# Slots found per 128 with the one-hot matrix as the stationary side, and x stored to DRAM once, tile by tile

## The chip, the cores and the metric

One core of a Trainium2 chip runs the whole program. The metric is the device time of one execution in microseconds (us). The kernel before takes 1715.98 us, the median of three runs (1715.34 to 1718.17).

## The reference

Two transformer layers run one after the other on 512 tokens of width 1024, in fp32. The change touches only the end of the second layer, a mixture of 32 experts in 4 groups of 8. Each token goes to one group and to two experts of it:

```python
def hier_moe(h, w_rg, b_rg, w_re, b_re, w_g, w_u, w_d):
    g_logits = hf @ w_rg + b_rg
    _, g_sel = lax.top_k(g_logits, 1)
    ...
    top_val, top_idx = lax.top_k(e_logits_sel, EXPERT_TOPK)     # 2 of the group's 8
    e_weight = softmax(top_val) * g_weight
    gates = sum(one_hot(e_idx, 32) * e_weight)                  # [tokens, 32]
    ...
        hid = silu(hf @ w_g[e]) * (hf @ w_u[e]) * gates[:, e]   # [tokens, 256] for each expert e
        out = out + hid @ w_d[e]
```

The layer's result is x + hier_moe(rmsnorm(x)).

## The kernel before, in words

Everything ahead of the experts (mixers, feed-forward part, the projection `out_proj(w_o2)`) leaves x, 512 tokens of 1024 fp32 numbers, in SBUF as four tiles of 128 tokens (index t). `out_proj` works in two column halves c = 0 and 1. DVE adds each tile's result to x and DVE or ACT squares it (`xsq`, `xss`) for the norm. After a half, `logits(c)` (L1379) transposes x on TensorE, ACT copies the result out of PSUM (`xT`), and TensorE multiplies it with the router's weights (`psB`). At its end two DMAs of POOL's queue (L1394 and L1395) send the half, 1 MB each: one to `x3d`, a copy of x in DRAM that the experts' tokens are fetched from, and one to `out`, which the experts' results are added to later.

Then the pools of the projection are closed, `x` among them, and the room is given to expert weights and to the pool `fn3`, in which the router works. `norm_r` (L658) begins the router with `nv<-xss` on DVE and makes 1/rms (`rsy`); the router turns logits into two experts for each token and a place for each of its two choices (`dest`, L1510). 32 experts have 64 places each, 2048 places in all, worked on in 16 passes q of 128 places (two experts). Of every token the table `tab` (L1528, six columns per token and choice) holds token number, weight and 1/(2 rms). `ogd` (L1552) is a small table for a branch of overfull experts that is not taken here.

`experts` (L1554) then has these parts:

- `slots(c)` (L1578) finds for 256 places which token lies there. For every t DVE compares a row 0..255 (`io`) with `dest`, first for the one choice (`oa`, L215) and then for both (`oh`, L210): 0/1 matrices of 128 tokens by 256 places. TensorE multiplies `tab` (stationary, six columns) by them, ACT copies the 6x256 result (`s6`, printed as `s`), TensorE turns it into two 128x6 pieces, and DVE writes token number `si`, weight `wt` and scale `rs`.
- `gather(q)` (L1566): POOL's indirect DMA fetches 128 rows of `x3d` into `xg`. Two such buffers are cleared once ahead of it (L1562).
- `turn(q)`: eight transposes of `xg` on TensorE (`pslin`, L242), which DVE spreads into `XT` (L207).
- `up(q)` (L1608): 32 matmuls `psA<-gu,XT`; ACT and DVE then make the hidden values `th`.
- `down(q)` (L1619): two transposes of `th` (`pspr<-cc,th`), ACT copies them (`hT`), 16 matmuls `psB<-dn,hT`, copies `y`, and POOL's indirect DMA adds `y` to `out` (L1632).

The engines run their instructions in the order in which the code issues them. Ahead of the loop stand slots(0), gather(0), gather(1), slots(1), turn(0), gather(2). A round q of the loop (L1641) is up(q), turn(q+1), gather(q+3), down(q-1), and in every second round slots(q/2 + 2) at its end.

Expert weights come over SP's queue in one fixed order: `gu` (1 MB each, four to a pass, 18 buffers, L1415) and `dn` (512 KB each, four to a pass, 6 buffers, L1420). A transfer into a used buffer waits on SP until the matmuls of its old content are done, dn number n for the down of number n-6, and whatever stands behind it on SP waits too.

Of the kernel before, what the change touches and what calls it, by code (L numbers as in the profile page):

```python
# [21 lines left out]
NT = 4  # L22
# [48 lines left out]
def constants():  # L71
    p = np.arange(128)
    t, q = p[:, None], p[None, :]
    same = (t // 64) == (q // 64)
    c = {"ident": np.eye(128), "t128": t <= q}
    t64, q64 = t % 64, np.arange(64)[None, :]
    c1 = {"tri": same & (t <= q), "gc": np.concatenate([t % 64 < q % 64, t % 64 <= q % 64], axis=1)}
    for l, n in SOLVE:
        b = 2 ** (l - 1)
        near = t64 // (b << n) == q64 // (b << n)  # L80
        c1["lv%d" % l] = near & ((t64 // b < q64 // b) if l == 1 else (t64 // b > q64 // b))
    c1["blk"] = same
    c1["id64"] = (t % 64) == np.arange(64)[None, :]
    c1["hsel"] = (t // 64) == np.arange(2)[None, :]
    tt = 128 * (3 - np.arange(4))[None, :, None] + p[:, None, None]
    c5 = {}
    c5["cm"] = ((tt - 16 * np.arange(31)[None, None, :] - 31) >= 0).reshape(128, 124)
    c2 = {}
    for l in range(7):
        n = 2 ** l  # L90
        c2["sl%d" % n] = (t // (2 * n) == q // (2 * n)) & (t % (2 * n) < n) & (q % (2 * n) >= n)
    c4 = {"up": np.where(q > t, -BIG, 0.0)}
    c3 = {"io": np.broadcast_to(np.arange(256)[None, :], (128, 256)), 
          "tok": t + 128 * np.arange(4)[None, :] + 1,
          "ts128": t < q, "ps64": np.broadcast_to(64.0 * (16 * (np.arange(32) // 16) + 2 * (np.arange(32) % 8) + np.arange(32) // 8 % 2)[None, :], (128, 32)),
          "rv": np.broadcast_to(8.0 - np.arange(8)[None, :], (128, 8))}
    out = {}
    for name, d in (("cc", c), ("cc1", c1), ("cc2", c2), ("cc3", c3), ("cc4", c4), ("cc5", c5)):
        at, parts = 0, []
        for k, v in d.items():  # L100
            v = np.asarray(v, np.float32)
            CCOL[k] = (name, at, v.shape[1])
            at += v.shape[1]
            parts.append(v)
        out[name] = np.concatenate(parts, axis=1)
    dist = 511 - np.arange(1024)
    bk = t5_thresholds()[np.clip(dist, 0, 511)]
    oh = np.zeros((33, 1024), np.float32)
    ok = (dist >= 0)
    oh[bk[ok], np.nonzero(ok)[0]] = -1.0  # L110
    oh[32, ~ok] = BIG
    sel = np.zeros((8, 4, 128), np.float32)
    for i in range(4):
        sel[2 * i, i, :64] = 1
        sel[2 * i + 1, i, 64:] = 1
    out["onehot"] = oh
    out["sel8"] = sel.reshape(8, 512)
    return out
# [70 lines left out]
class Kern:  # L189
# [1171 lines left out]
    def moe(self):  # L1361
        nc, tc, I = self.nc, self.tc, self.I
        with ExitStack() as s3:
# [5 lines left out]
            with tc.tile_pool(name="x3p", bufs=1) as xp:  # L1369
# [3 lines left out]
                nc.gpsimd.dma_start(bb, I["b_rt"].to_broadcast([128, 36]))  # L1373
                self.tt(wr, wr, self.pc("n2", 0, 8)[:, :, None].to_broadcast([128, 8, 36]))
                x3 = self.x
                ov = self.out.rearrange("(t p) d -> p t d", p=128)
                Lg = xp.tile([128, NT, 36], F32, name="Lg")

                def logits(c):  # L1379
                    psr = self.pt("B")  # L1380
                    for t in range(NT):
                        ps = self.pt("A")
                        for k in range(4):
                            self.tr(ps[:, k * 128:(k + 1) * 128], x3[:, t, (4 * c + k) * 128:(4 * c + k + 1) * 128])
                        xT = xp.tile([128, 4, 128], F32, name="xT", tag="xT", bufs=2)
                        self.copy("a", xT, ps.rearrange("p (k t) -> p k t", k=4))
                        for k in range(4):
                            self.mm(psr[:, t * 36:(t + 1) * 36], xT[:, k, :], wr[:, 4 * c + k, :], k == 0, k == 3)
# [2 lines left out]
                        self.copy("v", Lg, p3)  # L1391
                    else:
                        self.tt(Lg, p3, Lg, ALU.add)
                    for d in (self.x3d.rearrange("(t p) d -> p t d", p=128), ov):  # L1394
                        nc.gpsimd.dma_start(d[:, :, c * 512:(c + 1) * 512], x3[:, :, c * 512:(c + 1) * 512])  # L1395

                ss = self.out_proj(I["w_o2"], self.oT, xp, after=logits)
                self.dump("x3", x3)
                self.expert_load(2)
                self.rstack.close()  # L1400
                self.mw.append(L("mw2", side="right"))
# [151 lines left out]

    def experts(self, me):  # L1554
        nc = self.nc
        si = me.tile([128, 16], I32, name="si")
        wt = me.tile([128, 16], F32, name="wt")
        rs = me.tile([128, 16], F32, name="rs")
        TH, XT = {}, {}
        xg = [me.tile([128, D], F32, name="xg%d" % j) for j in range(2)]  # L1560
        for x in xg:
# [13 lines left out]
                        self.tr(ps[:, k * 128:(k + 1) * 128], xg[q % 2][:, (4 * c + k) * 128:(4 * c + k + 1) * 128])  # L1575
                    self.spread(XT[q], ps, c)

        def slots(c):  # L1578
            if c > 7:
                return  # L1580
            dc = me.tile([128, 2, NT], F32, name="dc", tag="dc", bufs=2)
            self.ts(dc, self.dest, -256.0 * c, None, op0=ALU.add)
            oh = [[None] * NT, [None] * NT]
            for t in range(NT):
                a = me.tile([128, 256], F32R, name="oa", tag="oa", bufs=2)
                self.ts(a, self.cc("io"), dc[:, 0, t:t + 1], None, op0=ALU.is_equal)
                o = me.tile([128, 256], F32R, name="oh", tag="oh", bufs=4)
                self.stt(o, self.cc("io"), dc[:, 1, t:t + 1], a.bitcast(F32), ALU.is_equal, ALU.add)
                oh[0][t], oh[1][t] = a, o
            ps = self.pt()  # L1590
            for k in range(2):
                for t in range(NT):
                    self.mm(ps[0:6, 0:256], self.tab[:, k, t, :], oh[k][t], k == 0 and t == 0, k == 1 and t == NT - 1)
            s6 = me.tile([6, 256], F32, name="s6", tag="s6", bufs=1)
            self.copy("a", s6, ps[0:6, 0:256])
            ps = self.pt()
            for q in range(2):
                self.tr(ps[:, q * 6:q * 6 + 6], s6[:, q * 128:(q + 1) * 128])
            qs = slice(2 * c, 2 * c + 2)
            st = me.tile([128, 2, 6], F32, name="st", tag="st", bufs=2)  # L1600
            self.copy("v", st, ps[:, 0:12].rearrange("p (q f) -> p q f", q=2))
            self.tt(rs[:, qs], st[:, :, 3], st[:, :, 4], ALU.add)
            self.tt(wt[:, qs], st[:, :, 1], st[:, :, 2], ALU.add)
            e = me.tile([128, 2], F32, name="e2", tag="e2", bufs=2)
            self.ts(e, st[:, :, 0], 0.0, 1.0e5, ALU.is_equal, ALU.mult)
            self.stt(si[:, qs], st[:, :, 0], -1.0, e, ALU.add, ALU.add)

        def up(q):  # L1608
            ps = self.pt("A")
# [22 lines left out]
            nc.gpsimd.indirect_dma_start(out=self.out, out_offset=bass.IndirectOffsetOnAxis(ap=si[:, q:q + 1], axis=0),  # L1632
                                         in_=y, in_offset=None, bounds_check=T - 1, oob_is_err=False, compute_op=ALU.add)

        slots(0)
        gather(0)
        gather(1)
        slots(1)
        turn(0)
        gather(2)  # L1640
        for q in range(16):  # L1641
            up(q)
            self.expert_load(3, 4 * q + 4, 4 * q - 4)
            turn(q + 1)
            gather(q + 3)
            if q:
                down(q - 1)
                self.expert_load(3, 4 * q + 4, 4 * q)
            if q % 2 == 0:
                slots(q // 2 + 2)  # L1650
        down(15)

    def spread(self, dst, ps, c):
# [55 lines left out]
```

## Time and profile before

| | us |
|---|---|
| median of three runs | 1715.98 |
| the profiled execution | 1718.04 |
| its span in the trace | 1716.3 |
| expert stage: first matmul of up(0) to end of the last weight transfer | 1465.75 to 1689.31 |
| TensorE busy | 1575.3 (92% of the span) |
| DVE busy | 938.0 (55%) |
| all DMA engines, mean over the span | 136 GB/s |

Times inside the execution are us from the span's start. PE is TensorE, SP the engine that issues weight transfers. The queue q1 carries the transfers that SP issues, q0 those of POOL. Names such as `oa`, `th` or `gu` are the program's tiles, and `r` is any of the router's small tiles; `L238` and the like are often lines of a helper (matmul, transpose, copy), so that a tile's name tells more than its line.

### The profile page before, as it was taken

Reading aid. Unit: us, or ns where it says so; the run is one execution under the profiler, and the core shown is the slowest. Engines: PE = TensorE matmul, PEld = TensorE weight load, DVE = VectorE, ACT = ScalarE, POOL = GpSimd, SP = SyncE. Lnnn points to the kernel's source line nnn. Section 1 sums busy time; section 2 is a strip of 40 time slices with the busy share of each in tenths; the row PEclk is TensorE's granted clock in tenths of the full one; section 3 lists DMA queues with packets and bytes.
Section 4 is the critical chain, followed back from the end, with each engine's and each line's share of the span. In section 5 each row is a group of like instructions: output and inputs, shape, how many; then the busy total and the mean of one; then the engine's idle time right before and its main releaser. Section 6 shows DMA issues by size and latency. Waiting matters only on the chain. (4 is left out here: it accounts for less than half of the span.)

```text
span 1716.3 us, 25176 instructions
## 1 busy us (share of the span) xinstructions
PE 1575.3 (92%) x9529; PEld 1108.7 (65%) x9529; DVE 938.0 (55%) x2227; ACT 558.4 (33%) x1130; POOL 297.5 (17%) x237
## 2 busy tenths in 40 slices
PE   6999999998899999999999999689888995999986
PEld 4678687868666678888888887467665473333321
DVE  4666766136587443877777234498487625323210
ACT  3432322334344333444444232334333431111100
POOL 3520101523111143000000000132032032212111
PEclk7899999999799999999999999799999997999998
DMA  5110111632221342222223333522212276799996
GB/s 185 58 60 15 52 60 48 212 102 68 83 74 53 104 158 88 92 93 97 94 93 94 96 92 94 149 72 94 68 38 69 111 266 264 275 366 367 409 401 215
DMA packets 88326, 233.06 MB, mean 136 GB/s; under 512 B 12131, under 2 KB 16707, under 8 KB 79756
## 3 DMA queue, kind: packets, MB, share of 16 engines
q1 hardware_dynamic: 78464, 206.70, 34.6%
q0 software_dynamic: 5856, 12.83, 2.8%
q10 hardware_dynamic: 3884, 11.91, 2.0%
q8 instruction: 76, 1.25, 0.3%
q14 instruction: 46, 0.38, 0.1%
HBM read 216.90 MB, written 22.09 MB: 139 GB/s over the span
## 5 line engine op out<-in xcount | busy, mean ns | idle before, releaser
L207 POOL TENSOR_TENSOR lo<-raw,hi 128x512 fp32r<-128x512 f32 (+1 forms) x152 | 199.3, 1314 | 994.7 <-ACT hi L219 891.5
L219 ACT ACTIVATE hi<-raw 128x512 fp32r<-128x512 f32 (+1 forms) x314 | 197.5, 631 | 432.7 <-PE pslin L238 193.1
L238 PE MATMUL pslin<-hhi,hi 128*128 128x512 f32 x696 | 281.9, 405 | 3.4 <-ACT hi L219 3.4
L238 PE MATMUL pslin<-hhi,lo 128*128 128x512 f32 x696 | 281.6, 405 | 1.5 <-POOL lo L207 1.5
L238 PE MATMUL pslin<-hlo,hi 128*128 128x512 f32 x696 | 282.4, 406 | 0.0
L207 DVE TENSOR_TENSOR lo<-raw,hi 128x512 fp32r<-128x512 f32 x162 | 111.3, 687 | 116.1 <-ACT hi L219 115.6
L238 PEld LDWEIGHTS pslin<-hhi,lo 128*128 128x128 f32 x696 | 132.7, 191 | 36.9 <-issue 3.7
L238 PEld LDWEIGHTS pslin<-hhi,hi 128*128 128x128 f32 x696 | 132.9, 191 | 35.7 <-ACT hi L219 4.3
L238 PEld LDWEIGHTS pslin<-hlo,hi 128*128 128x128 f32 x696 | 132.7, 191 | 32.5 <-issue 3.1
L238 PE MATMUL psA<-gu,XT 128*64 128x512 f32 x512 | 127.0, 604 | 12.7 <-DMA gu<-in_egu_dram 12.0
L238 PEld LDWEIGHTS psA<-gu,XT 128*64 128x64 f32 x512 | 37.9, 138 | 88.4 <-issue 63.1
L238 PE MATMUL psB<-dn,hT 128*64 128x512 f32 x256 | 72.4, 602 | 5.9 <-ACT hT L201 3.8
L210 DVE SCALAR_TENSOR_TENSOR u<-lr,pcol,u 128x511 f32<-128x511 f32 x88 | 65.9, 749 | 8.2 <-ACT u L219 6.6
L207 DVE TENSOR_TENSOR lr<-pslin,Rb 128x512 f32<-128x512 f32 x54 | 37.3, 690 | 51.3 <-PE pslin L238 44.0
L238 PE MATMUL pslin<-lo,hhi 128*128 128x512 f32 (+1 forms) x144 | 54.8, 381 | 2.9 <-DVE lo L207 2.8
L238 PE MATMUL pspr<-hi,hhi 128*128 128x512 f32 (+1 forms) x144 | 54.7, 382 | 1.7 <-ACT hq L219 1.7
L238 PE MATMUL pslin<-hi,hhi 128*128 128x512 f32 (+1 forms) x144 | 55.6, 387 | 0.0
L210 DVE SCALAR_TENSOR_TENSOR th<-th,psA 128x256 f32<-128x256 f32 x16 | 6.7, 418 | 88.5 <-ACT th L219 88.5
L238 PE MATMUL pspr<-lo,hhi 128*128 128x512 f32 (+1 forms) x144 | 54.3, 377 | 0.0
L238 PE MATMUL pspr<-hi,hlo 128*128 128x512 f32 (+1 forms) x144 | 54.2, 376 | 0.0
L238 PE MATMUL pslin<-hi,hlo 128*128 128x512 f32 (+1 forms) x144 | 53.9, 375 | 0.0
L219 ACT ACTIVATE th<-psA,rs 128x256 f32<-128x256 f32 x16 | 7.6, 474 | 136.6 <-PE psA L238 136.6
(652 smaller groups left out, 3046.6 us busy)
## 6 DMA issues: line engine op xcount, KB each, us to landing
gu<-in_egu_dram SPq DMA_DIRECT2D x64, 1024.0 KB, 16.1
dn<-in_ed_dram SPq DMA_DIRECT2D x64, 512.0 KB, 9.5
raw<-in_w_up_dram SPq DMA_DIRECT2D x88, 256.0 KB, 2.6
raw<-in_w_dn_dram SPq DMA_DIRECT2D x44, 256.0 KB, 2.6
raw<-in_w_g_dram SPq DMA_DIRECT2D x32, 256.0 KB, 2.6
raw<-in_w_o_dram SPq DMA_DIRECT2D x32, 256.0 KB, 2.7
raw<-in_w_a_dram SPq DMA_DIRECT2D x32, 256.0 KB, 2.6
raw<-in_w_rw_dram SPq DMA_DIRECT2D x28, 256.0 KB, 2.6
```

The source lines that it names most:

```text
L207: return (eng or self.nc.vector).tensor_tensor(out, a, b, op=op)
L210: return self.nc.vector.scalar_tensor_tensor(out, a, s, b, op0=op0, op1=op1)
L219: return self.nc.scalar.activation(out, in_, f, **k)
L238: return self.nc.tensor.matmul(out, lhsT=lhsT, rhs=rhs, start=start, stop=stop)
```

## The change

The x stores become eight ACT DMAs of one 128x512 tile each, issued inside `logits` ahead of that tile's transposes, and they go to `x3d` alone. `out` is filled once after `out_proj` by a DMA of POOL's queue from `x3d` (DRAM to DRAM, 2 MB). `slots(q)` now works for one pass of 128 places: the one-hot matrix (128x128) is the stationary side and `tab`'s six columns are the moving side, so that the result has places on the partitions and DVE reads it from PSUM with no copy and no transposes. The tiles of `slots` (`dc`, `oa`, `oh`, `e2`, `st`, `si`, `wt`, `rs`) move from the pool `me`, which is opened at the experts' start, to the pool `mh`, which is older and lies on the other side. In the loop `slots(q+3)` stands right behind `turn(q+1)` in every round up to q = 12; three of them stand ahead of the loop.

```diff
-    c3 = {"io": np.broadcast_to(np.arange(256)[None, :], (128, 256)), 
+    c3 = {"io": np.broadcast_to(np.arange(128)[None, :], (128, 128)),
...
                 def logits(c):
                     psr = self.pt("B")
                     for t in range(NT):
+                        nc.scalar.dma_start(self.x3d[t * 128:(t + 1) * 128, c * 512:(c + 1) * 512], x3[:, t, c * 512:(c + 1) * 512])
                         ps = self.pt("A")
...
-                    for d in (self.x3d.rearrange("(t p) d -> p t d", p=128), ov):
-                        nc.gpsimd.dma_start(d[:, :, c * 512:(c + 1) * 512], x3[:, :, c * 512:(c + 1) * 512])
 
                 ss = self.out_proj(I["w_o2"], self.oT, xp, after=logits)
+                nc.gpsimd.dma_start(self.out, self.x3d)
...
-        si = me.tile([128, 16], I32, name="si")
+        mh = self.mh
+        si = mh.tile([128, 16], I32, name="si")
...
-        def slots(c):
-            if c > 7:
+        def slots(q):
+            if q > 15:
                 return
-            dc = me.tile([128, 2, NT], F32, name="dc", tag="dc", bufs=2)
-            self.ts(dc, self.dest, -256.0 * c, None, op0=ALU.add)
+            dc = self.dest
+            if q:
+                dc = mh.tile([128, 2, NT], F32, name="dc", tag="dc", bufs=2)
+                self.ts(dc, self.dest, -128.0 * q, None, op0=ALU.add)
+            ps = self.pt()
             for t in range(NT):
-                a = me.tile([128, 256], F32R, name="oa", tag="oa", bufs=2)
+                a = mh.tile([128, 128], F32R, name="oa", tag="oa", bufs=2)
...
+                self.mm(ps[:, 0:6], a, self.tab[:, 0, t, :], t == 0, False)
+                self.mm(ps[:, 0:6], o, self.tab[:, 1, t, :], False, t == NT - 1)
-            for k in range(2):
-                for t in range(NT):
-                    self.mm(ps[0:6, 0:256], self.tab[:, k, t, :], oh[k][t], k == 0 and t == 0, k == 1 and t == NT - 1)
-            s6 = me.tile([6, 256], F32, name="s6", tag="s6", bufs=1)
-            self.copy("a", s6, ps[0:6, 0:256])
...
+            self.ts(e, ps[:, 0:1], 0.0, 1.0e5, ALU.is_equal, ALU.mult)
+            self.stt(si[:, c], ps[:, 0:1], -1.0, e, ALU.add, ALU.add)
...
-        slots(0)
-        gather(0)
-        gather(1)
-        slots(1)
+        for q in range(3):
+            slots(q)
+            if q < 2:
+                gather(q)
...
             turn(q + 1)
+            slots(q + 3)
             gather(q + 3)
...
-            if q % 2 == 0:
-                slots(q // 2 + 2)
```

Three places of the program show what moves. The first is DVE's order between the projection and the router. `xsq` is the norm's square of the last tile, `nv` the router's first operation, and DMAHW names completion counters of transfers that ACT and SP issue. Before:

```order
L207 TENSOR_TENSOR x<-pspr,x 128x512 [waits PE_49]
L651 ISA xsq,xss<-x 128x512 [waits DVE_49]
L651 ISA xss 128x1
L207 TENSOR_TENSOR nv<-xss 128x4 [waits DVE_49,Activation_49]
L1461 MEMSET r_12979 128x128
L216 TENSOR_SCALAR nv<-nv 128x4 [waits DVE_49]
L203 CAST r_12979<-cc_12492 128x128
```

The same place now:

```order
L207 TENSOR_TENSOR x<-pspr,x 128x512 [waits PE_49]
L651 ISA xsq,xss<-x 128x512 [waits DVE_49]
L651 ISA xss 128x1
L207 TENSOR_TENSOR Lg<-psB,Lg 128x144 [waits PE_49]
L207 TENSOR_TENSOR nv<-xss 128x4 [waits DMAHW2_49,DMAHW4_49,DMAHW1_49,DMAHW6_49,DMAHW0_49,DMAHW7_49,DVE_49,Activation_49]
L1460 MEMSET r_12984 128x128
L216 TENSOR_SCALAR nv<-nv 128x4 [waits DVE_49]
```

`nv` has gained waits on six DMA counters, and the addition of the logits' two halves (`Lg`) has come to stand ahead of it.

The second place is POOL's order from the x stores to the first gather. DMASW names counters of POOL's own transfers. Before:

```order
L1395 DMA x3d<-x 128x4x512 [waits DVE_49]
L1395 DMA out_dram<-x 128x4x512
L1493 MEMSET r_13019 128x32 [waits DVE_49,Activation_49]
L1552 DMA ogd<-r_13073 128x32x4 [waits DVE_49]
L1562 MEMSET xg_13086 128x1024 [waits DMASW2_49,DMASW1_49,DMASW3_49,DMASW0_49,DMASW4_49,PE_49,DMASW5_49,Activation_49,Pool_49]
L1562 MEMSET xg_13087 128x1024
L1566 DMA xg_13086<-x3d,si 128x1024 [waits DVE_49,Pool_49]
```

The same place now:

```order
L1397 DMA out_dram<-x3d 32x16384 [waits DMAHW4_49,DMAHW6_49,DMAHW2_49,DMAHW7_49,DMAHW1_49,DMAHW0_49]
L1492 MEMSET r_13024 128x32 [waits DVE_49,PE_49,Activation_49]
L1551 DMA ogd<-r_13078 128x32x4 [waits DVE_49]
L1562 MEMSET xg_13091 128x1024 [waits DMASW0_49,PE_49,DMASW1_49,Activation_49,Pool_49]
L1562 MEMSET xg_13092 128x1024
L1566 DMA xg_13091<-x3d,si 128x1024 [waits DVE_49,Pool_49]
```

The two stores have gone; one copy waits for the six counters that `nv` waits for, and the clearing of `xg` waits for fewer transfers.

The third place is TensorE's order between up and down of a loop round. `pslin<-cc,xg` are the transposes of turn, `pspr<-cc,th` those in front of down, and `pspr` with `oa` or `oh` the matmuls of slots. Before, in a round with slots:

```order
L242 MATMUL pslin<-cc,xg_13087 128x128 [waits PE_49]
L242 MATMUL pslin<-cc,xg_13087 128x128 x3
L242 MATMUL pspr<-cc,th 128x128 x2
L238 MATMUL pspr<-oa,r_13055 6x256 [waits PE_49]
L238 MATMUL pspr<-oa,r_13055 6x256
L238 MATMUL psB<-dn_13406,hT 64x512 [waits DMAHW1_49,Activation_49]
```

Now, in every round:

```order
L242 MATMUL pslin<-cc,xg_13092 128x128 [waits PE_49]
L242 MATMUL pslin<-cc,xg_13092 128x128 x3
L238 MATMUL pspr<-r_13060,oa 128x6 [waits DVE_49]
L238 MATMUL pspr<-r_13060,oh 128x6 [waits DVE_49]
L238 MATMUL pspr<-r_13060,oa 128x6
L238 MATMUL pspr<-r_13060,oh 128x6 [waits DVE_49]
L242 MATMUL pspr<-cc,th 128x128 [waits DVE_49,PE_49]
L242 MATMUL pspr<-cc,th 128x128
L238 MATMUL psA<-gu_13596,XT 64x512 [waits DMAHW6_49,DVE_49]
L238 MATMUL psB<-dn_13496,hT 64x512 [waits DMAHW2_49,Activation_49]
L238 MATMUL pspr<-r_13060,oa 128x6 [waits DVE_49]
L238 MATMUL pspr<-r_13060,oh 128x6 [waits DVE_49]
```

The transposes of `th` stood directly behind those of `xg`; four matmuls of slots, three of them with a wait for DVE, now stand between the two, and the other four lie among the first matmuls of down. On DVE the loop's new order is `th`, `XT`, `th`, `XT`, then `oa` and `oh` for t = 0 to 3.

## Rows read from the trace of the kernel before

**Rows 1.** Chain of waits, 1425 to 1475: start us, length us, what ran or landed.

```profile
1430.87 19.55 DMA out_dram<-x
...
1458.63 4.16 DMA xg<-x3d,si
...
1465.75 7.07 PE psA L238 x32
```

**Rows 2.** The same chain, 1540 to 1717.

```profile
1563.43 1.99 PE psB L238 x8
...
1567.69 18.06 DMA gu<-in_egu_dram
...
1672.89 16.38 DMA gu<-in_egu_dram
...
1689.31 3.22 PE psA L238 x13
```

**Rows 3.** DVE timeline: start us, length us, engine, line, operation, tiles, [idle before, releaser].

```profile
1430.64 0.16 DVE L207 TENSOR_TENSOR nv<-xss 128x4 f32<-128x4 f32 x1
...
1432.62 0.16 DVE L210 SCALAR_TENSOR_TENSOR rst<-rst,nv 128x4 f32<-128x4 f32 x1
...
1435.51 0.31 DVE L207 TENSOR_TENSOR Lg<-Lg,rsy 128x144 f32<-128x144 f32 x1
...
1444.01 0.42 DVE L1510 TENSOR_REDUCE r<-r 128x8 f32<-128x256 f32 x1
...
1450.55 1.00 DVE L215 TENSOR_SCALAR dc<-r 128x8 f32<-128x8 f32 x2 [4.62 <-DMA out_dram<-x]
```

**Rows 4.** POOL timeline, same columns.

```profile
1446.22 1.70 POOL L1552 DMA_DIRECT2D ogd<-r  x1 [14.47 <-DVE r L207]
1450.56 1.88 POOL L1562 MEMSET xg<- 128x1024 f32 x2 [2.64 <-DMA out_dram<-x]
```

**Rows 5.** Transfers issued from 1420 to 1460: count, KB each, us from issue to landing.

```profile
x3d<-x POOLq DMA_DIRECT2D x1, 1024.0 KB, 13.2
```

**Rows 6.** The page's transfers of 128x512 weights over the whole span, same columns.

```profile
raw<-in_w_up_dram SPq DMA_DIRECT2D x88, 256.0 KB, 2.6
```

**Rows 7.** DMA queues from 1440 to 1445: packets, MB, share of 16 engines' time.

```profile
q1 hardware_dynamic: 191, 1.42, 67.0%
q0 software_dynamic: 188, 0.71, 34.6%
```

**Rows 8.** PE timeline of two loop rounds, columns as in rows 3.

```profile
1493.68 1.09 PE L242 MATMUL pslin<-cc,xg 128*128 128x128 f32 x8
1494.61 0.38 PE L242 MATMUL pspr<-cc,th 128*128 128x128 f32 x2
...
1495.52 3.65 PE L238 MATMUL psB<-dn,hT 128*64 128x512 f32 x16 [0.30 <-ACT hT L201]
...
1500.88 0.28 PE L242 MATMUL pspr<-cc,s 6*128 6x6 f32 x2
...
1508.11 1.09 PE L242 MATMUL pslin<-cc,xg 128*128 128x128 f32 x8
...
1520.40 1.09 PE L242 MATMUL pslin<-cc,xg 128*128 128x128 f32 x8
```

**Rows 9.** DVE timeline of the first of these rounds.

```profile
1494.30 0.42 DVE L210 SCALAR_TENSOR_TENSOR th<-th,psA 128x256 f32<-128x256 f32 x1 [6.66 <-ACT th L219]
...
1496.23 0.60 DVE L215 TENSOR_SCALAR oa<-cc,dc 128x256 fp32r<-128x256 f32 x2
1496.75 0.87 DVE L210 SCALAR_TENSOR_TENSOR oh<-cc,dc,oa 128x256 fp32r<-128x256 f32 x2
```

**Rows 10.** Chain of waits, 1475 to 1500: the first psB of down(0).

```profile
1483.22 3.65 PE psB L238 x16
```

**Rows 11.** Stretches: us; busy (count) of PE, PEld, DVE, ACT, POOL; PEclk, DMA share, GB/s.

```profile
1493.70:1508.10 14.40, 14.10 (x70) 5.26 (x68) 6.17 (x19) 1.83 (x4) 2.61 (x2) 1.00 1.01 363
1567.70:1689.30 121.60, 106.92 (x444) 35.59 (x440) 24.76 (x58) 11.32 (x24) 17.66 (x13) 0.99 1.02 401
```

More of the change, by code (lines that the diff above doesn't have):

```diff
@@ L1375, in moe @@
                 x3 = self.x
-                ov = self.out.rearrange("(t p) d -> p t d", p=128)
                 Lg = xp.tile([128, NT, 36], F32, name="Lg")
@@ L1555, in experts @@
         nc = self.nc
-        si = me.tile([128, 16], I32, name="si")
-        wt = me.tile([128, 16], F32, name="wt")
-        rs = me.tile([128, 16], F32, name="rs")
+        mh = self.mh
+        si = mh.tile([128, 16], I32, name="si")
+        wt = mh.tile([128, 16], F32, name="wt")
+        rs = mh.tile([128, 16], F32, name="rs")
         TH, XT = {}, {}
@@ L1576, in turn @@
                     self.spread(XT[q], ps, c)
-        def slots(c):
-            if c > 7:
+        def slots(q):
+            if q > 15:
                 return
-            dc = me.tile([128, 2, NT], F32, name="dc", tag="dc", bufs=2)
-            self.ts(dc, self.dest, -256.0 * c, None, op0=ALU.add)
-            oh = [[None] * NT, [None] * NT]
-            for t in range(NT):
-                a = me.tile([128, 256], F32R, name="oa", tag="oa", bufs=2)
[L1586 to L1590, printed above, removed]
-            for k in range(2):
-                for t in range(NT):
-                    self.mm(ps[0:6, 0:256], self.tab[:, k, t, :], oh[k][t], k == 0 and t == 0, k == 1 and t == NT - 1)
-            s6 = me.tile([6, 256], F32, name="s6", tag="s6", bufs=1)
-            self.copy("a", s6, ps[0:6, 0:256])
[L1596 to L1606, printed above, removed]
@@ new lines, in slots @@
+            dc = self.dest
+            if q:
+                dc = mh.tile([128, 2, NT], F32, name="dc", tag="dc", bufs=2)
+                self.ts(dc, self.dest, -128.0 * q, None, op0=ALU.add)
+            io = self.cc("io")
+            ps = self.pt()
+            for t in range(NT):
+                a = mh.tile([128, 128], F32R, name="oa", tag="oa", bufs=2)
+                self.ts(a, io, dc[:, 0, t:t + 1], None, op0=ALU.is_equal)
+                o = mh.tile([128, 128], F32R, name="oh", tag="oh", bufs=4)
+                self.stt(o, io, dc[:, 1, t:t + 1], a.bitcast(F32), ALU.is_equal, ALU.add)
+                self.mm(ps[:, 0:6], a, self.tab[:, 0, t, :], t == 0, False)
+                self.mm(ps[:, 0:6], o, self.tab[:, 1, t, :], False, t == NT - 1)
@@ L1608, in up @@
+            e = mh.tile([128, 1], F32, name="e2", tag="e2", bufs=2)
+            c = slice(q, q + 1)
+            self.ts(e, ps[:, 0:1], 0.0, 1.0e5, ALU.is_equal, ALU.mult)
+            self.stt(si[:, c], ps[:, 0:1], -1.0, e, ALU.add, ALU.add)
+            st = mh.tile([128, 4], F32, name="st", tag="st", bufs=2)
+            self.copy("v", st, ps[:, 1:5])
+            self.tt(rs[:, c], st[:, 2:3], st[:, 3:4], ALU.add)
+            self.tt(wt[:, c], st[:, 0:1], st[:, 1:2], ALU.add)
         def up(q):
```

## The prediction

> **What bounds the kernel now.** I read the chain of waits first, backwards from its end. From 1567.69 on it is nothing but weight transfers of `gu`, one after the other, seven from the first to the last row shown, until 1689.3 [rows 2]. In that stretch the DMA engines are busy throughout (share 1.02, 401 GB/s) although TensorE also looks busy [rows 11]: the last ten passes run at the pace of the weights. The mean of a round there is (1689.31 - 1585.75) / 6 = 17.26 us, where 1585.75 is the landing of the first, 1567.69 + 18.06 [rows 2]. What starts that stretch is the down matmul of pass 6 at 1563.43, which frees the buffers that SP's queue has been waiting for [rows 2].
>
> Before it TensorE sets the pace. A pair of loop rounds takes 1520.40 - 1493.68 = 26.72 us, 13.36 each; the round with slots takes 14.43, the one without 12.29 [rows 8]. Yet the DMA share is 1.01 in one of these rounds too [rows 11], so the two limits lie close together there. That is the doubt in everything below.
>
> The stage's start hangs on another transfer. DVE idles 4.62 us until `out_dram<-x` has landed [rows 3], a DMA of 19.55 us in the chain; the first gather follows at 1458.63 and the first expert matmul at 1465.75 [rows 1].
>
> So the change is worth what it does to the chain from router to up(0), and to the time from up(0) to the down of pass 6. What it does behind pass 6 weighs nothing as long as a round of TensorE stays under 17.26.
>
> **The start.** The wait for `out_dram<-x` goes: the slots' tiles no longer lie where x was. But the pool that grew shifts the router's pool onto x instead. The new DVE order shows it: `nv`, the router's first operation, now waits for the counters of the x stores. It ran at 1430.64, directly after the last square [rows 3]. Everything behind it on DVE, which is the whole router, waits as well; POOL's copy to `out` waits for the same stores.
>
> When do they land? The last is issued by about 1432 (ACT takes its turns between the copies `xT`). From below: a 256 KB transfer takes 2.6 us where nothing competes [rows 6], 1434.5. From above: the 1 MB store of x took 13.2 us in the same place, beside weights [rows 5], 1445.3. I take the middle, 1440: weights start again just then, but the first stores of the half leave before them. What competes is seen in [rows 7]: in five us the two queues moved almost equally many packets, 191 and 188, and the queue with the larger packets got twice the bytes, 1.42 against 0.71 MB.
> The Trainium skill, "DMA: Bandwidth & Descriptors", section "Queues, rings and completion order", says that each DMA engine takes turns between its queues packet by packet. The counts of 191 and 188 agree. The rule speaks against this change: stores in rows of 2 KB would get a smaller share beside weights than the packets of 3.8 KB did (0.71 MB / 188); by it 1 MB at 37.6 packets a us takes 13.6 us, the stores land near 1443, and the sum below would be about 3 us worse.
>
> From `nv` at 1440 to the scaling of the logits are 2.36 us (2.0 to the last step shown, two more at 0.2) [rows 3], so 1442.4 instead of 1435.51, 6.9 late. `dest` then ends at 1444.43 + 6.9 = 1451.3. Slots(0) starts without waiting, between the router's last operations: 1.5 us of these (from 1444.43 to where the idle began, 1450.55 - 4.62 = 1445.93), eight comparisons, and one more us for the last matmul, `e` and `si`. At 256 wide the eight take 4 x (0.30 + 0.44) = 2.9 us by the pairs in [rows 9]; at 128 wide between a half and the whole, I take 2.3. `si` is there at about 1456.1, and POOL's issue at about 1457. POOL itself must first issue `ogd` and clear `xg`, 1.70 + 1.88 us [rows 4], behind a router that ends at about 1452.8: 1456.4, just in time. Gather(0) is thus about 1.5 us earlier than 1458.63, and up(0) with it: **-1.5**. With the bounds of the stores, 5.5 earlier and 5.3 later: -7.0 to +3.8. The new 2 MB copy to `out` must have landed ahead of the gathers of the same queue at the worst; it starts near 1441 and weights stop soon after 1450, so I take nothing for it; uncovered it is up to 3 us, within the upper bound.
>
> **The loop up to pass 6.** Slots no longer stands behind down but between the transposes of turn and those of `th`, in every round. TensorE works in order: four small matmuls there wait for comparisons, and the transposes of `th`, ready long ago, wait behind them. Before, psB began 1495.52 - 1493.68 = 1.84 us after the last up matmul [rows 8]. DVE can begin `oa` only 1496.23 - 1493.68 = 2.55 us after it, since `th`, `XT`, `th`, `XT` come first [rows 9]. Two `oa` and two `oh` take 0.52 + 0.87 = 1.4 us at 256 wide [rows 9], 0.7 if halved; I take 0.95, so 3.5. Then the last small matmuls, 0.07 each by the spacing of the nearest rows, two transposes of 6x6 that end 0.28 after the start with some 0.21 each [rows 8], 0.14 together. From there the old path: 1495.52 - 1494.61 = 0.91 from transposes to psB [rows 8]. psB begins 4.55 after up instead of 1.84: +2.7.
> The other four small matmuls cost 0.3 and a short wait of 0.1 inside down; a psA matmul now fills 0.2 of the wait for `hT`. What goes is the old slots, 14.43 - 12.29 = 2.14 in every second round, 1.07 a round. Sum of a round: 2.7 + 0.3 + 0.1 - 0.2 - 1.07 = **+1.8**, to 15.2 us. From psB of pass 0 at 1483.22 [rows 10] to that of pass 6 are six rounds: **+10.8**. Bounds: +1.2 a round if the comparisons cost half and the other small matmuls nothing, +3 if they stay as long as at 256 wide and down waits for the last four as well.
> In front of this, round 0 has slots(3) between turn(1) and up(1); its last comparisons come 2.3 us behind `XT`, of which the first psA matmuls cover about one: **+1.3**. Down(0) gets the first delay of its kind, with no old slots to set against it: **+2.7**.
>
> **The rest.** The first psB of pass 6 starts at 1563.43 - 1.5 + 1.3 + 2.7 + 10.8 = 1576.7, 13.3 late. Weights were behind TensorE there: from psB to the first landing are 1585.75 - 1563.43 = 22.3 us [rows 2], where an empty queue would need one round of 17.26 and about one us to issue, 18.3. Up to 4.0 of lag can thus be caught up while TensorE is slower; I take **-3**. From there the weights' pace is the same in both, since 15.2 is under 17.26. The ACT stores (eight issues), the POOL issues saved and the copies `s` saved lie on engines that wait here.
>
> Sum: -1.5 + 1.3 + 2.7 + 10.8 - 3 = +10.3 on the profiled execution of 1718.04, which is its span of 1716.3 and 1.7 around it: 1728.3. The median of the runs lies 2.06 under that execution, so **1726.3**.
>
> **Rivals.**
> - *Transfers bind from the start.* The DMA share of 1.01 before pass 6 [rows 11] speaks for it: a later TensorE would then only use up a lag. Against it: a round there is 13.36 us for 4 MB and a late one 17.26 for 6 MB, 3.3 against 2.9 us a MB, so some of the engines' time goes to gathers and added rows or is slack. The end moves with the start alone: 1715.98 - 1.5 = 1714.5, no change.
> - *Faster, through the start.* If the stores land as if alone, by 1434.5, up(0) starts 7.0 earlier; weights begin to flow again when its buffers come free, so all transfers shift, and the loop's delay is covered as in the first rival. 1709. It decides from about 1437.5 on (3.5 us or more won at up(0)), and only if transfers bind before pass 6. For it: DMA was idle just before 1430. Against it: weights restart there, and [rows 7].
> - *Slower still.* Stores land at 1445.3 and a round loses 3: 3.8 + 1.3 + 2.7 + 18 - 3 = +22.8, 1738.8. The packets of [rows 7] speak for the first half, nothing shown for the second.
> - *The wait has only moved* (the change doesn't take out what it means to): stores at 1445.3, loop as forecast, 1726.3 + 5.3 = 1731.6; part of the forecast's own range.
>
> **Chances.** What a measurement here can tell from no change is about 0.2%, 3.4 us: 1712.6 to 1719.4. Forecast and its own spread (1719.5 to 1734): 0.62. Transfers bind: 0.16, no change. Faster through the start: 0.11. Slower still: 0.11. So faster 0.12 (with some of the first rival's lower edge), same 0.17, slower 0.71. The range 1712 to 1736 leaves out most of the third rival and about half of the last.
>
> **What would show it.** Right: `nv` begins with an idle stretch put down to the x3d stores, at 1437 to 1445; no idle on DVE ahead of the first `oa`; up(0) within 3 us of 1465.75; psB 4 to 5 us behind the last psA of up in rounds 1 to 12, with idle of TensorE put down to `oa` or `oh`; rounds of 14.5 to 16 us; from pass 6 on the old 17.26. Wrong: `th`'s transposes not held up, rounds still near 13.4 (then the comparisons come earlier on DVE than I think), a DMA share that stays at 1.0 in those rounds with the end unmoved (transfers bind), or up(0) moved by more than 5 us.

## The result, and the profile after

The changed kernel takes 1725.52 us, the median of six runs (1723.85 to 1729.85); the kernel before, run beside it, 1714.97 (1713.02 to 1718.17). The ratio is 1.0062 [1.0048, 1.0077], some 10.6 us slower. Run again beside other experiments it was 1.0078 [1.0059, 1.0098].

The two profiled executions differ by less, spans of 1722.1 and 1716.3, and the reason must be known before any row is compared. The last addition to x, DVE's row just ahead of the last square, begins at 1429.12 before and at 1419.43 after:

```profile
1429.12 0.69 DVE L207 TENSOR_TENSOR x<-pspr,x 128x512 f32<-128x512 f32 x1
```

```profile
1419.43 0.69 DVE L207 TENSOR_TENSOR x<-pspr,x 128x512 f32<-128x512 f32 x1
...
1424.95 0.31 DVE L207 TENSOR_TENSOR Lg<-psB,Lg 128x144 f32<-128x144 f32 x1 [4.11 <-PE psB L238]
1429.04 0.16 DVE L207 TENSOR_TENSOR nv<-xss 128x4 f32<-128x4 f32 x1 [3.78 <-DMA dn<-in_ed_dram]
```

Most of the 9.7 us between them is the spread of executions: in a second trace of the unaltered kernel before (e12) the row stands at 1421.57,

```profile
1421.57 0.69 DVE L207 TENSOR_TENSOR x<-pspr,x 128x512 f32<-128x512 f32 x1
```

and in the other eleven anywhere from 1419.4 to 1427.4. A small part belongs to the change, whose stores of the first column half stand ahead of this row: from the last addition of the first half to that of the second it is 28.1 us in the four traces that store x on POOL and 27.5 in the ten that store it on ACT. In this pair of traces the 9.7 us hide most of the loss. All times below are therefore counted from the start of this row, called x. From x to the end of the span it is 1716.3 - 1429.1 = 287.2 us before (288.8 in the repeat) and 302.7 after (301.1 in the repeat): 12 to 15.5 us lost behind x.

The rows also show the new wait: after the last square DVE idles, but for one addition (`Lg`), until `nv` at x + 9.6, against x + 1.5 before [rows 3]. The trace names a weight transfer as the releaser, which landed at that moment; the last store of x, issued at 1421.98, had landed 6.8 us later, at 1428.8. In the repeat the trace names the store.

The chain from there to the first expert matmuls, after (start, length, what):

```profile
1447.29 6.99 DMA xg<-x3d,si
1454.41 1.94 PE pslin L242 x8
1456.36 8.52 PE psA L238 x32
```

The gather is issued at x + 27.9 (before: x + 29.5 [rows 1]), lands after 7.0 us instead of 4.2, and up(0) lasts 8.5 instead of 7.1; the last of these is no effect of the change, since it lasts 8.5 in the repeat of before as well (e12). The transfer of x to `out`, 19.55 us of the old chain, has gone from it.

A loop round of TensorE after, the counterpart of [rows 8]:

```profile
1489.71 1.09 PE L242 MATMUL pslin<-cc,xg 128*128 128x128 f32 x8
1490.56 0.25 PE L238 MATMUL pspr<-r,oa 128*128 128x6 f32 x1
...
1491.00 0.44 PE L242 MATMUL pspr<-cc,th 128*128 128x128 f32 x2
1491.40 1.07 PE L238 MATMUL psA<-gu,XT 128*64 128x512 f32 x2
1492.31 1.02 PE L238 MATMUL psB<-dn,hT 128*64 128x512 f32 x2
1493.26 0.27 PE L238 MATMUL pspr<-r,oa 128*128 128x6 f32 x1
...
1493.68 1.08 PE L238 MATMUL psB<-dn,hT 128*64 128x512 f32 x4
1494.69 0.27 PE L238 MATMUL pspr<-r,oh 128*128 128x6 f32 x1
1494.90 2.36 PE L238 MATMUL psB<-dn,hT 128*64 128x512 f32 x9
1496.67 0.64 PE L238 MATMUL psA<-gu,XT 128*64 128x512 f32 x1
1497.09 0.59 PE L238 MATMUL psB<-dn,hT 128*64 128x512 f32 x1
1497.15 7.40 PE L238 MATMUL psA<-gu,XT 128*64 128x512 f32 x29
1504.48 0.33 PE L242 MATMUL pslin<-cc,xg 128*128 128x128 f32 x1
```

The round is 14.77 us and has no idle row. psB begins 2.60 us behind the last psA of up, not 4.55. What is new is how the stream of up and down is cut: psA in runs of 2, 1 and 29 instead of 32, psB in 2, 4, 9 and 1 instead of 16, with small matmuls between. What that costs, and why, is worked out under e4.

The end of the chain after, as [rows 2]:

```profile
1571.67 17.54 DMA gu<-in_egu_dram
...
1678.57 17.34 DMA gu<-in_egu_dram
```

From pass 6 on it is again weights, (1695.91 - 1589.22) / 6 = 17.8 us a round (17.5 in the repeat; before 17.26, and 17.1 in its repeat).

Counted from x, worked out from each trace's rows (us; e1 to e12 are the experiments below):

| kernel | nv | gather(0) issued | up(0) | psB of pass 0 | psB of pass 6 | round | end of span |
|---|---|---|---|---|---|---|---|
| before | 1.5 | 29.5 | 36.6 | 54.1 | 134.3 | 13.37 | 287.2 |
| before, repeat (e12) | 1.5 | 28.9 | 36.2 | 55.2 | 135.4 | 13.37 | 288.8 |
| after | 9.6 | 27.9 | 36.9 | 58.1 | 146.8 | 14.77 | 302.7 |
| after, repeat (e8) | 10.6 | 28.8 | 37.6 | 58.4 | 147.1 | 14.78 | 301.1 |
| e1 stores alone | 1.5 | 26.1 | 35.8 | 55.3 | 135.5 | 13.36 | 287.7 |
| e2 slots alone | 1.5 | 25.7 | 34.5 | 54.9 | 143.6 | 14.77 | 298.6 |
| e3 tiles in me | 1.5 | 22.8 | 34.7 | 56.5 | 145.2 | 14.77 | 300.8 |
| e4 slots behind down | 10.3 | 28.5 | 39.7 | 60.9 | 138.8 | 12.98 | 293.8 |
| e5 copy behind gathers | 10.6 | 28.8 | 37.9 | 58.7 | 147.3 | 14.78 | 303.0 |
| e6 all three | 1.5 | 22.8 | 33.7 | 55.7 | 133.6 | 12.98 | 290.2 |
| e7 and cleared on DVE | 1.5 | 22.6 | 34.4 | 56.5 | 134.4 | 12.98 | 290.3 |
| e9 slots(q+3) behind down | 1.5 | 22.6 | 33.7 | 54.3 | 132.3 | 12.98 | 292.9 |
| e10 and useless matmuls | 1.5 | 22.6 | 37.6 | 57.0 | 134.9 | 12.98 | 294.7 |
| e11 before, slots moved | 1.5 | 29.2 | 36.6 | 54.2 | 132.3 | 13.02 | 288.9 |

### The profile page after: what moved, and what is told of

It reads as the page before. It is cut to its first block, busy times and chain, and to the rows that moved or that the text cites. A ratio compares the mean times of both kernels' runs of the same rounds, so it can differ in the third digit from the quotient of the medians.

```text
span 1722.1 us, 25404 instructions
## 1 busy us (share of the span) xinstructions
PE 1581.9 (92%) x9573; PEld 1121.4 (65%) x9577; DVE 950.6 (55%) x2338; ACT 555.3 (32%) x1122; POOL 294.7 (17%) x234
## 5 line engine op out<-in xcount | busy, mean ns | idle before, releaser
L238 PEld LDWEIGHTS pslin<-hhi,lo 128*128 128x128 f32 x696 | 132.3, 190 | 37.8 <-POOL lo L207 3.8
L238 PE MATMUL psA<-gu,XT 128*64 128x512 f32 x512 | 135.1, 603 | 12.4 <-DMA gu<-in_egu_dram 12.1
L238 PEld LDWEIGHTS psA<-gu,XT 128*64 128x64 f32 x512 | 41.8, 138 | 85.4 <-issue 63.5
L238 PE MATMUL psB<-dn,hT 128*64 128x512 f32 x256 | 80.6, 615 | 0.9 <-ACT hT L201 0.8
L238 PE MATMUL pspr<-lo,hhi 128*128 128x512 f32 (+1 forms) x144 | 54.3, 377 | 0.0
```

The lines of the kernel that those rows point to most:

```text
L238: return self.nc.tensor.matmul(out, lhsT=lhsT, rhs=rhs, start=start, stop=stop)
```

## The experiments

**e1, the store part alone.** The old slots with its tiles in the old pool, with the ACT stores and the copy to `out`. The edit against the kernel before, shortened:

```diff
+ nc.scalar.dma_start(self.x3d[...], x3[:, t, ...])      # in logits, per t
- for d in (self.x3d..., ov): nc.gpsimd.dma_start(d[...], x3[...])
+ nc.gpsimd.dma_start(self.out, self.x3d)
```

> The kernel before with the store part alone: x goes to x3d in eight ACT stores, out is copied from x3d; slots is the old one, its tiles in the old pool. Theory A (the loss is TensorE's, in the new slots): the router starts unheld, slots(0) waits for the x stores alone, which have landed when dest is there, so up(0) begins 3 to 6 us earlier against the last square of x; rounds stay at 13.36 us; time 2 to 6 us under before, 1709 to 1713. Theory B (the loss is in the transfers: stores beside weights, and a 2 MB copy that slows the weights and the gathers): 3 us or more over before, 1718 to 1724.

Measured: 1714.23, ratio 1.0003 [0.999, 1.0016]. Neither: no loss, no gain. The first gather is issued 2.8 to 3.4 us earlier than in the two traces of before, but lands after 6.6 us, and up(0) is 0.4 to 0.8 earlier; by psB of pass 0 nothing is left.

**e2, the slots part alone**, tiles in `me`, x stored by POOL as before. The edit against the changed kernel, shortened:

```diff
- nc.scalar.dma_start(self.x3d[...], x3[:, t, ...])
+ for d in (self.x3d..., ov): nc.gpsimd.dma_start(d[...], x3[...])
- mh = self.mh
+ mh = me
```

> The kernel before with the slots part alone: 128 places at a time, one-hot stationary, behind turn in every round, its tiles in the old pool me; x is stored as before by POOL. Theory A: a round takes 14.7 to 14.8 us instead of 13.36 and psB of pass 6 comes about 12 us later than before, counted from the last square of x; time 1725 to 1730. Theory B: rounds may grow, but the end moves by less than 4 us, 1715 to 1719, since the loss was in the transfers.

Measured: 1728.54, ratio 1.0090 [1.0067, 1.0114]; rounds of 14.77, psB of pass 6 8 to 9 us late from x, the end 10 to 11. The loss is here. Theory B, the transfers, falls with these two runs.

**e3, the changed kernel with the tiles of slots back in `me`** (`mh = me` in `experts`, one line).

> The changed kernel with the tiles of slots back in the pool me, nothing else. The router's pool then no longer lies on x: nv begins directly behind the last square (in the changed kernel it idled 3.8 us by its trace). Theory A and the prediction's step on the start: dest comes about 5 us earlier (limited by the addition of the logits), up(0) and the end 4 to 5 us earlier than the changed kernel, 1719 to 1722. Rival: the first gather is held by the copy to out in the same queue whatever DVE does; then less than 2 us is won, 1724 to 1726.

Measured: 1727.0, ratio 1.0080 [1.0064, 1.0097]. The wait of `nv` is gone and the gather is issued 5.0 us earlier than after, yet it lands after 9.4 us, and up(0) gains 2.2 of the 5; the end from x gains 1.8 on the first trace and 0.3 on the repeat. By time nothing is won. The router's new wait was real and nearly free.

**e4, slots behind down.**

```diff
-        for q in range(3):
+        for q in range(4):
             slots(q)
...
             turn(q + 1)
-            slots(q + 3)
             gather(q + 3)
             if q:
                 down(q - 1)
+            slots(q + 4)
```

> The changed kernel with slots(q+4) behind down(q-1) at the end of a round instead of slots(q+3) behind turn, and four slots ahead of the loop. Four small matmuls then stand behind the transposes of th, in the wait for hT, and four behind all 16 psB; no pair of psA or psB is broken up. Theory A, with a part of the loss in broken pairs: a round takes 13.3 to 14.0 us instead of 14.77, time 1717 to 1721. Rival 1 (the eight matmuls themselves cost it all): 14.5 to 14.8, time unchanged at 1724 to 1727. Rival 2 (the step of the prediction, now real: they wait for the comparisons and hold psB): rounds over 15, time over 1727.

Measured: 1719.63, ratio 1.0031 [1.0018, 1.0044], half of the loss gone; what is left begins ahead of the rounds, where up(0) comes 3 us later from x than before. The round is 12.98, below what theory A allowed for and below the old kernel's. The same eight small matmuls now lie in two places:

```profile
1507.48 0.38 PE L242 MATMUL pspr<-cc,th 128*128 128x128 f32 x2
1507.62 0.25 PE L238 MATMUL pspr<-r,oa 128*128 128x6 f32 x1
...
1508.40 3.65 PE L238 MATMUL psB<-dn,hT 128*64 128x512 f32 x16 [0.19 <-ACT hT L201]
1511.98 0.27 PE L238 MATMUL pspr<-r,oa 128*128 128x6 f32 x1
...
1512.52 7.09 PE L238 MATMUL psA<-gu,XT 128*64 128x512 f32 x32
1519.54 0.66 PE L242 MATMUL pslin<-cc,xg 128*128 128x128 f32 x4
```

Start to start: psB to the small ones 3.58, psA to the next round 7.02, together 10.60. In the round of after above the same 48 matmuls take 0.91 + 0.95 + 1.01 + 2.25 + 7.33 = 12.45. That difference of 1.85 is the whole difference of the rounds (1.79).

The starts of the single matmuls inside these rows show where it lies. In a long run the 64-column matmuls of psA and psB start two at a time, 6 to 57 ns apart, and a new pair every 0.43 us; `up` and `down` issue them in turn for the two experts of a pass. In the round of after eight of the 48 start alone, with 0.43 to 0.52 us to the next start: the first two psA, the two psB behind them, and the last four psA before the next round. In the same 1.9 us run eight matmuls in the middle of psA in e4, and four at the end of psA after:

```profile
1515.15 1.89 PE L238 MATMUL psA<-gu,XT 128*64 128x512 f32 x8
```

```profile
1502.67 1.88 PE L238 MATMUL psA<-gu,XT 128*64 128x512 f32 x4
```

A matmul without a partner thus takes some 0.43 us where half a pair takes 0.215, and eight of them are 1.7 of the 1.85 us. From psB of pass 0 to that of pass 6, 48 start alone after (88.65 us), 12 before (80.21, four in each round with slots) and none in e4 (77.91). Which expert each of them belongs to the trace doesn't say, so that two psA that start ahead of psB leave their partners over at the end of the round is argued, not shown.

**e8, the changed kernel once more.**

> The changed kernel once more, unaltered, beside the next three on one chip. All theories: 10 to 14 us over before, 1724 to 1728; counted from the last addition to x, psB of pass 6 at 146 to 148 and the end at 299 to 304 as in its first trace (146.75 and 302.65), whatever the part before does. If that part alone is 5 us or more shorter than in the kernel before again, the change reaches further back than I think.

Measured: 1728.03, ratio 1.0078 [1.0059, 1.0098]; the loss lies behind x again.

**e5, the copy to `out` behind the gathers.**

```diff
-                nc.gpsimd.dma_start(self.out, self.x3d)
...
         gather(2)
+        with self.tc.issue_after(self.last.ins):      # behind gather(2) on POOL
+            nc.gpsimd.dma_start(self.out, self.x3d)
```

> The changed kernel with the 2 MB copy to out queued on POOL behind gather(2) instead of ahead of the gathers; nothing else. Theory A (the copy holds the first gather in their common queue: it landed 7.0 us after its issue, and 4.2 in the kernel before): gather(0) lands in 4 to 4.5 us, up(0) 2.5 to 3 us earlier from the last addition to x, the end with it, 1721 to 1723. Rival (the gather is slow for another reason, weights in flight): landing stays near 7, time as the changed kernel.

Measured: 1726.03, ratio 1.0073 [1.0048, 1.0098]. The copy was issued at 1459.35, after the first gather had landed, and that still took 7 us:

```profile
1448.94 7.07 DMA xg<-x3d,si
```

Theory A fails here: the copy doesn't hold the gather. Nor do weights: in the changed kernel q1 moved no packet from 1447 to 1457. The first gather lands after 6.3 to 9.4 us in the ten traces that show its landing and have a part of the change in them, and after 4.2 (before and e12) and 4.5 (e11) in the other three.

The rows leave one candidate that no run tests: `ogd`, the 64 KB table for the branch that isn't taken, which goes out on the same queue of POOL ahead of the gather. After, it is issued at 1442.06, 5.2 us ahead of the gather; before, at 1446.22 [rows 4], 12.4 ahead. Its times from issue to landing, after and before:

```profile
ogd<-r POOLq DMA_DIRECT2D x1, 64.0 KB, 10.8
```

```profile
ogd<-r POOLq DMA_DIRECT2D x1, 64.0 KB, 12.0
```

So after the change `ogd` lands 5.6 us behind the gather's issue, and before 0.4 us ahead of it. In all ten traces that show both landings the gather is slow where `ogd` has 4.5 us or more still to go, and then lands 0.2 to 1.8 us behind it, and quick where `ogd` lands no more than 0.9 us after the gather's issue. In e3, where the gather was issued 5.0 us earlier and took 9.4, it lands 0.2 us behind `ogd`. No run moves `ogd` alone, so that it holds the gather is argued, not shown.

**e6, all three edits** (e3, e4 and e5).

> The changed kernel with three edits: slots behind down, the tiles of slots in the pool me, the copy to out behind gather(2). Theory A (each of the three was a loss of its own, and the new form of slots is the cheaper one): rounds of 12.9 to 13.1 us, gather(0) issued about 6.5 us earlier than in the kernel before and landed in 4.2, psB of pass 6 at 125 to 129 us from the last addition to x (before: 134.3), end 4 to 8 us under before, 1706 to 1710. Rival (before pass 6 the transfers bind as well, so an earlier TensorE only waits for weights): psB of pass 6 earlier, but the first landing behind it later by as much, time within 3 us of before, 1711 to 1716.

Measured: 1717.19, ratio 1.0012 [0.9993, 1.0032]. The rival holds: the time is 1.7 us over that of the kernel before beside it. psB of pass 6 comes 0.7 and 1.8 us earlier from x than in the two traces of before, the end 3.1 and 1.5 later. The chain is weights from 1548.35 on, x + 124 (in the repeat of before from x + 125), and up(0) lasted 9.6 us:

```profile
1457.68 9.62 PE psA L238 x32
```

```profile
1548.35 18.13 DMA gu<-in_egu_dram
```

**e7, `xg` cleared on DVE** (`nc.vector.memset` for `nc.gpsimd.memset` in e6).

> The kernel of the run before it with the two clearings of xg on DVE instead of POOL. In the traces so far DVE's first operation beside POOL's clearing lasts 2.9 us instead of 0.2 and ends with it. Theory (the two engines hold each other up there): the two clearings cost DVE 1 to 1.5 us, the first slots are done 1 to 2 us earlier, up(0) by as much, time 0 to 2 us under the run before. Rival (DVE's long operation has nothing to do with POOL): up(0) 1 us later.

Measured: 1713.75, ratio 0.9988 [0.9971, 1.0006], no change that can be told from before. In e6 two comparisons of DVE begin while POOL issues `ogd` and end with POOL's clearing (in the changed kernel it is `dc`, 2.91 us); in e7 the clearings take DVE 0.9 us each and the same comparisons are short. In e6:

```profile
1441.16 3.09 DVE L215 TENSOR_SCALAR oa<-cc,r 128x128 fp32r<-128x128 f32 x2
```

```profile
1442.25 1.86 POOL L1561 MEMSET xg<- 128x1024 f32 x2
```

e7:

```profile
1437.00 0.91 DVE L1561 MEMSET xg<- 128x1024 f32 x1 [0.16 <-issue]
...
1438.62 0.28 DVE L215 TENSOR_SCALAR oa<-cc,r 128x128 fp32r<-128x128 f32 x1
```

So DVE was held up beside POOL, as the theory says; but the first `si` came only 0.4 us earlier (x + 21.4 for 21.8), since DVE now does the clearing itself, and the gather then took 7.4.

**e9, slots(q+3) and then gather(q+3) behind down, none in round 0** (from e7).

```diff
             turn(q + 1)
-            gather(q + 3)
             if q:
                 down(q - 1)
-            slots(q + 4)
+                slots(q + 3)
+            gather(q + 3)
```

> The kernel of e7 with slots(q+3) and then gather(q+3) behind down(q-1), and none in round 0: up(1) is then not broken up by small matmuls. Theory A: from up(0) to psB of pass 0 takes 18 to 20 us instead of 22.1, rounds stay at 13.0, psB of pass 6 comes at 130 to 132 us from the last addition to x instead of 134.4. If transfers bind from there on, the end still moves by less than that: 1 to 2 us under e7, 1710 to 1714. Rival (TensorE binds before pass 6): the end comes 3 us or more earlier.

Measured: 1716.22, ratio 0.9998 [0.9981, 1.0016]. From up(0) to psB of pass 0 it took 20.6 us instead of 18 to 20; psB of pass 6 came at 132.3, within 0.3 of what was written, and the end at 292.9, 2.6 later than in e7 instead of earlier: four late gathers of 8.5 to 11.3 us now stand in the chain.

**e10, ten useless matmuls ahead of turn(0)** (from e9, results unread). turn(0) is held behind them, and slots(3) moves behind turn(0).

```diff
-        turn(0)
...
+            for k in range(10):
+                w = self.mm(ps, self.GU[0][:, 0, 0:128], self.GU[0][:, 1, :], k == 0, k == 9)
+        with self.tc.issue_after(w.ins):
+            turn(0)
+        slots(3)
```

> The kernel of e9 with ten matmuls of no use (128x512, results unread) put ahead of the first turn, where TensorE waits for the first gather. In the traces the granted clock there is 0.50, and up(0), which takes 7.1 us in the kernel before, took 8.0 to 9.6 in the runs with an earlier start. Theory (an idle TensorE starts up(0) at half clock, which eats a part of the earlier start): up(0) takes 7.0 to 7.5 us, psB of pass 0 comes 1.5 to 2.5 us earlier than in e9, time 0 to 2 us under it. Rival (up(0) is slow for late weights or a late XT): up(0) stays at 8 us or more.

Measured: 1717.97, ratio 1.0020 [1.0003, 1.0036]. That up(0) starts at the lower clock is borne out, the gain is not. In the changed kernel the granted clock is 0.50, the lower level of 1.2 GHz, in the stretch ahead of up(0), of which TensorE is busy for 4.82 of 8.30 us, 0.66 in the first half of up(0) and 1.00 after (stretch, busy of PE, PEld, DVE, ACT, POOL, clock, DMA share, GB/s):

```profile
1448.00:1456.30 8.30, 4.82 (x22) 4.55 (x22) 4.37 (x24) 0.00 (x0) 1.40 (x2) 0.50 0.41 69
1456.30:1460.60 4.30, 4.30 (x16) 1.42 (x16) 1.82 (x6) 0.00 (x0) 1.00 (x1) 0.66 0.24 67
1460.60:1464.90 4.30, 4.30 (x21) 1.27 (x18) 0.00 (x0) 0.00 (x0) 0.00 (x0) 1.00 0.58 177
```

e10, with the useless matmuls in 1448 to 1457, has up(0) at 1.00:

```profile
1457.30:1466.20 8.90, 8.90 (x38) 2.95 (x38) 3.12 (x15) 0.00 (x0) 1.56 (x2) 1.00 0.80 295
```

But the ten ended late and pushed up(0) from x + 33.7 to 37.6, and slots(3) then cut up(0) into three runs, so that it is still 8.9 long. That an earlier start is the reason for the lower clock falls with e12: there the start is that of before, and up(0) lasts as long as after:

```profile
1457.83 8.51 PE psA L238 x32
```

The 7.07 of [rows 1] is the shortest that any trace shows; e11 has it too.

**e11, the kernel before with its old slots moved behind turn.**

```diff
             turn(q + 1)
+            if q % 2 == 0:
+                slots(q // 2 + 2)
             gather(q + 3)
...
-            if q % 2 == 0:
-                slots(q // 2 + 2)
```

> The kernel before with its old slots(q/2+2) moved from the end of every second round to behind turn, the place of the changed kernel; nothing else. Theory (the place costs, whichever form slots has: what stands between the transposes of turn and those of th holds psB back): in a round with slots psB begins 3 us or more behind the last psA instead of 1.84, the mean round is 13.8 to 14.8 us instead of 13.36, time 1717 to 1725. Rival (only the new form loses there, by its stationary matrix of 128 columns): rounds of 13.3 to 13.5 us, time as before.

Measured: 1716.91, ratio 1.0021 [1.0003, 1.004], with a mean round of 13.02, under 13.37. Both expectations miss. psB does start late, 4.2 us behind the last psA of up, but six psA of the next pass fill that time:

```profile
1492.00 1.09 PE L242 MATMUL pslin<-cc,xg 128*128 128x128 f32 x8
...
1493.71 1.07 PE L238 MATMUL psA<-gu,XT 128*64 128x512 f32 x2
1494.72 0.28 PE L242 MATMUL pspr<-cc,s 6*128 6x6 f32 x2
...
1495.30 1.08 PE L238 MATMUL psA<-gu,XT 128*64 128x512 f32 x4
1496.21 3.60 PE L238 MATMUL psB<-dn,hT 128*64 128x512 f32 x16
1499.64 6.17 PE L238 MATMUL psA<-gu,XT 128*64 128x512 f32 x26
1505.74 1.09 PE L242 MATMUL pslin<-cc,xg 128*128 128x128 f32 x8
```

So it isn't the place as such. Here the 48 matmuls take 1.01 + 0.91 + 3.43 + 6.10 = 11.45, 0.85 over e4, and four of them start alone, the first two psA and the last two; 4 x 0.215 = 0.86. The changed kernel has eight alone and 1.85 over e4. That is what the new place costs: by how many matmuls lose their partner. A round with slots of the kernel before has four alone as well, and there TensorE idles another 0.30 us for `hT` [rows 8], which early psA fill here.

**e12, the kernel before, unaltered.**

> The kernel before, unaltered, for a second trace. If the place of the last addition to x, 1429.1 in its first trace and 1419.4 to 1427.4 in the others, is chance, it lies anywhere between 1418 and 1430; if the changed kernels are faster ahead of it, it lies at 1426 or later again. From there to the end: 286 to 289 us if the loss of 14 to 15.5 us behind x is the change's, 295 or more if the first trace of before was only lucky there.

Measured: 1712.08 (one run; the kernel before beside it 1712.84). x is at 1421.6, 7.5 us ahead of the first trace, with not one instruction changed; from x to the end 288.8, as expected if the loss is the change's.

## Why the prediction was right, and where it wasn't

The forecast, 1726.3, is 0.8 us from the median, and slower was given 0.71. Step by step, from x, as means of the two traces of each kernel:

- **The router's wait**: `nv` at x + 10.9 was forecast (1440), x + 9.6 and 10.6 were measured. The middle of the two bounds was right. The Trainium skill, "DMA: Bandwidth & Descriptors", section "Queues, rings and completion order", would by the use made of it have put `nv` at x + 13.9; the measurement decides, and it is earlier. Two things were left out. The first of the half's four stores went ahead of the weights and landed 2.0 us after its issue. And from 1423 to 1428 the stores' queue, q10, again moved about as many packets as that of the weights, but more of them than the 188 of [rows 7], beside weight packets half as large (1.34 MB / 360):

```profile
q1 hardware_dynamic: 360, 1.34, 70.2%
q10 hardware_dynamic: 323, 0.59, 30.8%
```

- **The start**: the gather was forecast 1.5 us earlier and was 0.9. up(0) was to be 1.5 earlier and was 0.9 later: a gather of 7 us instead of 4.2 was not foreseen (e5).
- **To psB of pass 0**: +1.3 and +2.7 were forecast behind up(0), 21.04 - 18.27 = 2.8 measured.
- **The round**: +1.8 was forecast, +1.4 measured, but the step that gives it failed: "four small matmuls there wait for comparisons", and psB 4.55 us behind up. It is 2.60. The `oa` and `oh` that follow `XT` on DVE are not t = 0 to 3 of one slots, as the order of instructions was read, but t = 2 and 3 of this one and then 0 and 1 of the next:

```profile
1505.33 0.25 PE L238 MATMUL pspr<-r,oa 128*128 128x6 f32 x1
```

```profile
1507.02 0.48 DVE L215 TENSOR_SCALAR oa<-cc,dc 128x128 fp32r<-128x128 f32 x2
1507.41 0.61 DVE L210 SCALAR_TENSOR_TENSOR oh<-cc,dc,oa 128x128 fp32r<-128x128 f32 x2
1508.34 0.51 DVE L215 TENSOR_SCALAR oa<-cc,dc 128x128 fp32r<-128x128 f32 x2 [0.32 <-PE pspr L238]
```

The matmul at 1505.33 runs 1.7 us before DVE's first comparison of its round at 1507.02: it reads what DVE wrote a round earlier, as it writes at 1508.34 for the next. The wait that stands in the order was long over. What costs in its place are eight matmuls of up and down that start without a partner, 1.7 us a round (e4, e11). Before it was four in every second round, so six more a round on average, 1.3 of the 1.4 us. For what the small matmuls do to those around them the prediction had only 0.3 + 0.1 - 0.2. That the round came out near the forecast is luck.
- **psB of pass 6**: 13.3 late forecast, 146.9 - 134.9 = 12.0 measured.
- **The lag**: -3 was forecast, and next to nothing was caught up. From psB to the first landing 1585.75 - 1563.43 = 22.3 us before became 1589.22 - 1566.18 = 23.0 (24.4 and 22.1 in the repeats). The 18.3 for an empty queue was an estimate that no row showed. The end from x is 301.9 - 288.0 = 13.9 late, not 10.3; of the 1.9 us behind pass 6 the spread between traces (17.1 to 17.8 a round) is as large.
- **The sum** comes nearer to the median than its terms to theirs: the medians lie 10.6 and 12.6 apart in the two sets, the traces 13.9 from x. The start and the lag, which were forecast as gains, and the two terms of TensorE, which were too large, cancel in part, and the kernels' times differ by 1.3 to 3.3 us less than the traces from x, 0.6 of it by the shorter way between the halves of x. To be 0.8 us from the median is luck.
- **Rivals**: "transfers bind from the start" was wrong for this change, since a slower TensorE was not hidden, but fits in the other direction: e6 and e11 bring psB of pass 6 forward by 1.2 and 2.6 us and end 2.3 and 0.9 later from x. The "faster" rival needed an early start; e3 issued the gather 6.4 us earlier than before and began up(0) only 1.7 earlier.

No kernel here is clearly faster than before; e7 is the nearest, 0.9988 [0.9971, 1.0006].

## What to carry to other kernels

A wait in the order of instructions is a question, not a cost: look which round wrote the operand before pricing it. Where matmuls run two at a time, count how many lose their partner when others come between them; the same eight small ones made a round 2.5 us longer than one without slots where eight matmuls lost theirs, and 0.7 where none did. And compare two profiled executions from a row close to the change: here chance ahead of it was nearly as large as the effect.

## What was not expected of the hardware

- The 64-column matmuls of up and down start in pairs, a pair every 0.43 us (32 in 7.02), and one that starts alone takes as long as a pair (e4).
- DVE operations of 0.2 to 0.3 us lasted 2.6 to 3.0 beside POOL's issue of `ogd` and its clearing of `xg` and ended with the clearing (after, e6); with the clearing on DVE they were short (e7).
- A gather of 128 rows took 4.2 to 4.5 us or 6.3 to 9.4, and the slow ones land just behind the table `ogd` of the same queue; whether that is the cause was not tested.
- The granted clock of the first half of up(0) was 1.00 in the first trace of before, in e11 and in e10, and 0.50 to 0.84 in the other eleven traces, the repeat of before among them (0.65): the same 32 matmuls lasted 7.1 and 8.5 us in the two traces of before, and 10.1 in e9.
